# A split-precision decoder trunk: high and low halves of x side by side in one 512-column operand

## The chip, the core and the metric

One core of one Trainium2 chip runs the whole kernel. The metric is the device time of one execution in microseconds (us); lower is better. The kernel before was timed three times: 864.3, 863.32 and 862.85 us, median 863.32.

## The reference

Two layers over 256 tokens of 1024 channels, all in float32. Cut to what matters here:

```python
for l in range(2):
    u = x @ w_in[l]                                   # 1024 -> 7168 columns
    u_conv, dq, dk, dv, mq, mk, mv, g = jnp.split(u, offs, axis=-1)
    y_a = conv_branch(u_conv, ...)                    # a*sigmoid(gt), 31-tap causal conv, layer norm, silu, @ w_conv_out
    y_b = diff_attention(dq, dk, dv, ...)             # rope on q and k, two softmaxes, rms norm, @ w_diff_out
    y_c = moba_attention(mq, mk, mv, ...)             # rope on q and k, softmax, @ w_moba_out
    gates = sigmoid(g + b_gate[l]).reshape(B, S, 3, D)
    m = gates[:, :, 0] * y_a + gates[:, :, 1] * y_b + gates[:, :, 2] * y_c
    x = layer_norm(ALPHA * x + m @ w_o[l], ...)
    h = square(relu(x @ w_ff1[l] + b_ff1[l]))         # 1024 -> 4096
    x = layer_norm(ALPHA * x + h @ w_ff2[l] + b_ff2[l], ...)
```

## The kernel before, in words

**Precision.** Every large product is made of three matmuls on halves: a value is split into a high part (rounded by a cast, on ScalarE) and a low part (the rest, a subtraction on VectorE), and `mm3` (line 391) adds low x high, high x low and high x high in one PSUM bank. Weights come from HBM in pieces of 128 x 1024 (512 KB) on SP's queue, and `Weights.get` (line 341) splits each: `raw` (4 buffers), `whi` and `wlo` (8 each).

**Units.** `tunit` (line 528) computes 256 output channels, channels on the partitions and tokens along the columns: two halves c, each one weight piece, each 8 steps over the input channels (kt). A step is one `mm3` with the weights loaded and x as the moving operand, 256 columns; both halves lie in one bank of tag `pm`. It is used for q and k (8 units in a layer), the gates (12) and most of MLP 1 (13, i from 3 to 15). The evictions: `rope` (line 602) copies four quarters of 32 partitions swapped to SBUF on ScalarE and multiplies and adds on VectorE; a gate takes two Tanh reads with bias; `hsplit` (line 860) two Relu reads with bias, a Square and a split.

**Order of a layer.** Convolution input, v projections, q and k, then the gates and output projections of the three branches in turn: gates and projection of the differential attention (bi 0), of MoBA (bi 1), of the convolution (bi 2); then `w_o` and layer norm 1, MLP 1 and MLP 2 interleaved, layer norm 2. VectorE does the 31 taps of the convolution meanwhile (`tap`, line 552). `conv_ln` (line 757: transposes, statistics, normalisation) stands behind the first gate unit of bi 2, `conv_silu` (line 775: transposes, scale and Tanh on ScalarE, product and split) behind the second. Attention pieces are put between the units by `tick`.

**Who sets the order.** All operations are recorded with guessed costs, and `Plan.order` (line 234) issues them engine by engine: of what could go at a moment, the one with the earliest due time, where due times follow TensorE's recorded order. Every instruction's line is therefore that of `record` (L122). PSUM has three tags: `pm` 2 banks, `pa` 4, `pt` 2.

Of the kernel before, what the change touches and what calls it, by code (L numbers as in the profile page):

```python
# [9 lines left out]
F32 = mybir.dt.float32  # L10
# [15 lines left out]
WARM = 4  # L26
NW = 8
CONV_BIAS = 0
BANKS = {"pm": 2, "pa": 4, "pt": 2}

NCOL = 24 + 4 * TAPS + 4 + 4 + 4 + 1 + 32
# [326 lines left out]
def kernel(ctx: ExitStack, tc: tile.TileContext, x, xT, w_in, w_p2, w_o, w_f1, w_f2,  # L358
# [38 lines left out]
    def at(pair, *ix):  # L397
        return tuple(a[ix] for a in pair)
# [11 lines left out]
    order = []  # L410
    for l in range(L):
        order += [w_in[l, i] for i in range(32)]
        for b in range(3):
            order += [w_in[l, 32 + 8 * b + i] for i in range(8)]
            order += [w_p2[l, 4 * b + i] for i in range(4)]
# [9 lines left out]
    X = [[], []]  # L425
    for h in range(2):
        a, hi, lo = slot(F32, "xt32"), slot(name="xh"), slot(name="xl")
        for q in range(2):
            s = slice(q * 512, (q + 1) * 512)
            R.SP.dma_start(a[:, s], xT[:, h * 1024 + q * 512:h * 1024 + (q + 1) * 512])  # L430
            split(hi[:, s], lo[:, s], a[:, s])
        X[0].append(hi)
        X[1].append(lo)
    cst_t = R.tile(const, [P, 896], F32, "cst", 1)
    R.SP.dma_start(cst_t, cst)
    cosT = cst_t[:, 0:256]
# [15 lines left out]
    def x_new():  # L452
        return [[slot(name="x") for _ in range(2)] for _ in range(2)]

    def x_at(X, kt, cols=slice(0, SEQ)):

        return tuple(X[i][kt // 4][:, (kt % 4) * SEQ + cols.start:(kt % 4) * SEQ + cols.stop]
                     for i in range(2))

    def rstd_of(var, n=1, eps=EPS, scale=1.0):  # L460

# [9 lines left out]
    def ln_tok(t, banks, resid, alpha, gb, dst, transposed):  # L471

        y = slot(F32, "y")
        st = R.tile(small, [P, 2, 6], F32, "st", 2)
        for h in range(2):
            s = slice(h * 512, (h + 1) * 512)
            R.DVE.scalar_tensor_tensor(y[:, s], in0=resid[:, s], scalar=alpha, in1=banks[h],
                                           op0=ALU.mult, op1=ALU.add)
            R.DVE.bn_stats(st[:, h, :], y[:, s])
        mv = col(2, "mv")  # L480
        R.DVE.bn_aggr(mv, st)
        rstd = rstd_of(mv[:, 1:2])
        for h in range(2):
            s = slice(h * 512, (h + 1) * 512)
            R.DVE.scalar_tensor_tensor(y[:, s], in0=y[:, s], scalar=mv[:, 0:1],
                                           in1=gb[0][:, s], op0=ALU.subtract, op1=ALU.mult)
            R.DVE.scalar_tensor_tensor(dst[:, s], in0=y[:, s], scalar=rstd,
                                           in1=gb[1][:, s],
                                           op0=ALU.mult, op1=ALU.add)
            if transposed is not None:  # L490
                ps = bank("pt")
                for k in range(4):
                    R.PE.transpose(ps[:, k * P:(k + 1) * P],
                                        dst[:, h * 512 + k * P:h * 512 + (k + 1) * P], ident)
                hi, lo = [transposed[i][h].rearrange("p (k n) -> p k n", k=4)[
                    :, :, t * P:(t + 1) * P] for i in range(2)]
                split(hi, lo, ps.rearrange("p (k n) -> p k n", k=4))

    def load_row(l, i):
        t = slot(F32, "rows")  # L500
# [3 lines left out]
    for l in range(L):  # L504
# [21 lines left out]


        def tunit(ticks=True):
            ps = bank()
            for c in range(2):  # L530
                w = W.get(k=KT)
                for kt in range(KT):
                    mm3(ps[:, c * 256:(c + 1) * 256], at(w, ALLP, kt), x_at(X, kt), kt == 0,
                        kt == KT - 1)
                if ticks:
                    tick()
            return ps

        attn = deque()
        tickn = [0]  # L540
# [61 lines left out]
        def rope(ps, dst):  # L602
            qq = R.tile(work, [P, 1024], F32, "zz", 3)
            q, qr = qq[:, :512], qq[:, 512:]
            for a in range(0, P, 64):
                R.Activation.copy(qr[a:a + 32], ps[a + 32:a + 64])
                R.Activation.copy(qr[a + 32:a + 64], ps[a:a + 32])
            p3 = ps.rearrange("p (c n) -> p c n", c=2)
# [191 lines left out]

        macc = [None, None]
        M = None
        for bi, gofs in ((0, 8), (1, 16), (2, 0)):
            sg = []
            for u in range(4):
                if u % 2 == 0:
                    sg.append(slot(F32, "sg"))
                ps = tunit()
                for c in range(2):
                    n = 2 * u + c  # L810
                    R.Activation.activation(sg[n // 4][:, (n % 4) * 256:(n % 4 + 1) * 256],
                                         ps[:, c * 256:(c + 1) * 256], AF.Tanh, scale=0.5,
                                         bias=half[:, C_BG + gofs + n:C_BG + gofs + n + 1])
                if bi == 2 and u == 0:
                    xn = conv_ln()
                if bi == 2 and u == 1:
                    conv_silu(xn)
            br = branch(bi)
            if bi == 2:
                M = x_new()  # L820
            for u in range(4):
                w = W.get(c=2, k=4)
                ps = bank()
                for c in range(2):
                    for kt in range(4):
                        mm3(ps[:, c * 256:(c + 1) * 256], at(w, ALLP, c, kt), at(br, ALLP, kt),
                            kt == 0, kt == 3)
                s = slice((u % 2) * 512, (u % 2 + 1) * 512)
                if bi == 0:
                    if u % 2 == 0:  # L830
                        macc[u // 2] = slot(F32, "macc")
                    a = macc[u // 2][:, s]
                    R.DVE.scalar_tensor_tensor(a, in0=sg[u // 2][:, s], scalar=1.0, in1=ps,
                                                   op0=ALU.add, op1=ALU.mult)
                else:
                    a, g = macc[u // 2][:, s], sg[u // 2][:, s]
                    R.DVE.scalar_tensor_tensor(g, in0=g, scalar=1.0, in1=ps, op0=ALU.add,
                                                   op1=ALU.mult)
                    R.DVE.tensor_add(a, a, g)
                    if bi == 2:  # L840
                        split(M[0][u // 2][:, s], M[1][u // 2][:, s], a, 0.5)
                tick()


        gb1 = load_row(l, 0), load_row(l, 1)
# [14 lines left out]
        def hsplit(i, ps):  # L860

            r = R.tile(work, [P, 1024], F32, "zz", 3)[:, :512]
            for c in range(2):
                n = 2 * i + c
                R.Activation.activation(r[:, c * 256:(c + 1) * 256], ps[:, c * 256:(c + 1) * 256],
                                     AF.Relu, bias=C[:, C_BF1 + n:C_BF1 + n + 1])
# [156 lines left out]
```

## Time and profile before

| what | value |
|---|---|
| median of three runs | 863.32 us |
| profiled execution | 864.63 us |
| its span, first to last instruction | 862.9 us |
| TensorE busy | 849.0 us (98%), 5736 matmuls |
| VectorE, ScalarE, GpSimd busy | 623.6, 513.0, 20.6 us |
| mean granted clock of TensorE | 0.998 |
| HBM traffic | 157.06 MB, mean 182 GB/s |

Engines are called PE (TensorE's matmuls), PEld (its weight loads), DVE (VectorE), ACT (ScalarE), POOL (GpSimd) and SP (the DMA queue). Matmuls overlap in their records: one of 256 columns has a record of 0.28 us, but in a run they start 0.12 us apart. The pace is therefore read from start to start, or from a run's length over its count. Busy times are shares of the whole span; what limits a stage is read in that stage.

### The profile page before, as it was taken

To read this page: it belongs to the slowest core of one execution; us is meant where nothing else is said; L and a number is where in the kernel's file an instruction comes from. 1 tells how busy PE (TensorE), PEld (TensorE's weight loads), DVE (VectorE), ACT (ScalarE), POOL (GpSimd) and SP (SyncE) were. 2 spreads that over 40 slices of the span, in tenths; PEclk is the share of its full clock that TensorE was granted. 3 is DMA by queue.
4 is the path that set the end of the run, shared out by engine and by line. 5 is a ranking of instruction groups with operands and counts; after the bars stand their busy time and mean duration, and the time that the engine had idled before them with its cause. 6 is when DMAs were issued, how large, how long until landed. Compare 5 with 4: busy or idle time off the path is not lost.

```text
span 862.9 us, 14667 instructions
## 1 busy us (share of the span) xinstructions
PE 849.0 (98%) x5736; PEld 779.1 (90%) x5736; DVE 623.6 (72%) x1011; ACT 513.0 (59%) x854; POOL 20.6 (2%) x26
## 2 busy tenths in 40 slices
PE   8999999999999999999999999999999999999996
PEld 7899999999988999999887999999998899999995
DVE  5899999985696654454688999998766874454445
ACT  5578997447347555555344688965472675555540
POOL 0000110000000000000000001000000000000000
PEclk9999999999999999999999999999999999999999
DMA  8874435565537765555265744355553686565521
GB/s 330 281 253 153 149 100 171 171 191 159 189 143 249 268 194 185 185 189 182 94 209 162 261 148 133 118 164 183 186 171 123 219 293 201 190 195 182 187 72 49
DMA packets 44421, 157.06 MB, mean 182 GB/s; under 512 B 4928, under 2 KB 5440, under 8 KB 44352
## 3 DMA queue, kind: packets, MB, share of 16 engines
q1 hardware_dynamic: 44352, 156.13, 54.4%
q8 instruction: 45, 0.74, 0.3%
q14 instruction: 24, 0.20, 0.1%
HBM read 155.06 MB, written 1.05 MB: 181 GB/s over the span
## 4 chain that ended last, share of the span: by engine, by line
PE 87%; DVE 7%; ACT 2%; DMA 2%; issue 1%; POOL 1%; DVEq 0%; ACTq 0%
PE pm L122 55%; PE pa L122 31%; ACT zz L122 2%; DVE wlo L122 2%; DVE big L122 1%; DVE zz L122 1%; DVE pt L122 1%; POOL col L122 1%; DMA raw<-in_w_f_dram 1%; DMA raw<-in_w_in_dram 1%; PE pt L122 1%; DVE qk L122 1%; ACT whi L122 0%; DMA big<-in_xT_dram 0%; DVE col L122 0%
## 5 line engine op out<-in xcount | busy, mean ns | idle before, releaser
L122 PE MATMUL pm<-big,whi 128*128 128x256 f32 x2496 | 452.6, 283 | 0.0
L122 DVE TENSOR_TENSOR wlo<-raw,whi 128x1024 fp32r<-128x1024 f32 (+1 forms) x283 | 341.4, 1210 | 153.6 <-ACT whi L122 152.1
L122 ACT CAST whi<-raw 128x1024 fp32r<-128x1024 f32 (+1 forms) x283 | 294.0, 1043 | 241.5 <-PE pm L122 170.8
L122 PEld LDWEIGHTS pm<-big,whi 128*128 128x128 f32 x2496 | 388.8, 192 | 1.2
L122 PE MATMUL pm<-big,wlo 128*128 128x256 f32 x1248 | 356.9, 286 | 0.0
L122 PEld LDWEIGHTS pm<-big,wlo 128*128 128x128 f32 x1248 | 239.0, 191 | 4.0 <-ACT pt L122 0.3
L122 PE MATMUL pa<-whi,big 128*128 128x512 f32 x704 | 224.8, 392 | 1.1 <-DVE big L122 1.1
L122 PEld LDWEIGHTS pa<-whi,big 128*128 128x128 f32 x704 | 132.8, 189 | 28.7 <-ACT whi L122 1.8
L122 PE MATMUL pa<-wlo,big 128*128 128x512 f32 x352 | 137.9, 392 | 0.0
L122 DVE SCALAR_TENSOR_TENSOR big<-hpad,half,big 128x256 f32<-128x256 f32 x240 | 103.3, 475 | 0.1
L122 PE MATMUL pm<-whi,big 128*128 128x512 f32 (+1 forms) x320 | 92.5, 370 | 0.0
L122 PEld LDWEIGHTS pa<-wlo,big 128*128 128x128 f32 x352 | 66.6, 189 | 12.7
L122 PEld LDWEIGHTS pm<-whi,big 128*128 128x128 f32 x320 | 58.3, 188 | 10.3 <-ACT zz L122 0.4
L122 PE MATMUL pm<-wlo,big 128*128 128x512 f32 (+1 forms) x160 | 59.3, 372 | 0.0
L122 ACT COPY zz<-pm 32x512 f32<-32x512 f32 (+1 forms) x72 | 40.8, 567 | 9.5 <-DVE zz L122 4.9
L122 DVE TENSOR_TENSOR big<-zz,big 128x512 fp32r<-128x512 f32 x32 | 22.1, 691 | 27.8 <-ACT big L122 27.8
L122 ACT ACTIVATE pt<-pt,col 128x256 f32<-128x256 f32 (+1 forms) x96 | 41.4, 459 | 0.7 <-DVE col L122 0.3
L122 POOL TENSOR_TENSOR col<-col,mhalf 128x1 f32<-128x1 f32 (+1 forms) x20 | 20.0, 1001 | 785.3 <-DVE col L122 785.3
L122 PEld LDWEIGHTS pm<-wlo,big 128*128 128x128 f32 x160 | 30.2, 189 | 4.8
L122 ACT CAST big<-pt 128x512 fp32r<-128x512 f32 x12 | 6.9, 591 | 37.7 <-PE pt L122 37.5
L122 DVE SCALAR_TENSOR_TENSOR big<-big,pa 128x512 f32<-128x512 f32 x16 | 11.0, 685 | 19.7 <-PE pa L122 19.5
L122 ACT ACTIVATE zz<-pm,cols 128x256 f32<-128x256 f32 x52 | 21.6, 465 | 4.7 <-PE pm L122 4.7
(79 smaller groups left out, 446.9 us busy)
## 6 DMA issues: line engine op xcount, KB each, us to landing
raw<-in_w_f_dram SPq DMA_DIRECT2D x128, 512.0 KB, 3.7
raw<-in_w_in_dram SPq DMA_DIRECT2D x109, 512.0 KB, 3.6
raw<-in_w_p_dram SPq DMA_DIRECT2D x24, 512.0 KB, 3.4
raw<-in_w_o_dram SPq DMA_DIRECT2D x16, 512.0 KB, 3.4
big<-in_rows_dram SPq DMA_DIRECT2D x10, 512.0 KB, 6.1
raw<-in_w_in_dram SPq DMA_DIRECT2D x6, 256.0 KB, 5.2
big<-in_xT_dram SPq DMA_DIRECT2D x4, 256.0 KB, 5.3
big<-in_x_dram SPq DMA_DIRECT2D x2, 512.0 KB, 8.2
```

The lines of the kernel that those rows point to most:

```text
L122: op.fn = lambda: fn(*args, **kw)
```

## The change

`x_new`, `x_at` and two new helpers lay x out so that for each kt the high and the low 256 columns stand side by side. In `tunit` a step becomes two matmuls: the high weights with all 512 columns (high and low x), and the low weights with the 256 high columns. The two halves of a bank are then added when they are read: `tsum` reads the upper half on ScalarE (with the bias) and adds the lower half on VectorE. Each half c of a unit takes a bank of its own, c = 0 of tag `pm`, c = 1 of `pt`. Relu and Tanh follow on the sum, 512 columns at a time. The gates of all branches stay recorded as before, but the order becomes gates 0, projection 0, gates 1, gates 2, `conv_ln`, projection 1 with `conv_silu` behind its second unit, projection 2. Weights are fetched in that order. The outputs of the splits after a norm and after the merge are written in two pieces or in three dimensions.

```diff
+GATED = (("gate", 0), ("out", 0), ("gate", 1), ("gate", 2), ("out", 1), ("out", 2))
...
+    def x_both(X, kt):
+
+        return X[kt // 2][:, (kt % 2) * 512:(kt % 2 + 1) * 512]
...
     for h in range(2):
-        a, hi, lo = slot(F32, "xt32"), slot(name="xh"), slot(name="xl")
+        a = slot(F32, "xt32")
         for q in range(2):
             s = slice(q * 512, (q + 1) * 512)
             R.SP.dma_start(a[:, s], xT[:, h * 1024 + q * 512:h * 1024 + (q + 1) * 512])
-            split(hi[:, s], lo[:, s], a[:, s])
+            split(*x_pair(X, 2 * h + q), a[:, s].rearrange("p (k n) -> p k n", k=2))
...
-                split(hi, lo, ps.rearrange("p (k n) -> p k n", k=4))
+                p4 = ps.rearrange("p (k n) -> p k n", k=4)
+                for j in range(2):
+                    split(*x_pair(transposed, 2 * h + j, slice(t * P, (t + 1) * P)),
+                          p4[:, 2 * j:2 * j + 2])
...
         def tunit(ticks=True):
-            ps = bank()
+            out = []
             for c in range(2):
                 w = W.get(k=KT)
+                ps = bank(("pm", "pt")[c])
                 for kt in range(KT):
-                    mm3(ps[:, c * 256:(c + 1) * 256], at(w, ALLP, kt), x_at(X, kt), kt == 0,
-                        kt == KT - 1)
+                    hi, lo = at(w, ALLP, kt)
+                    R.PE.matmul(ps, hi, x_both(X, kt), start=kt == 0, stop=False)
+                    R.PE.matmul(ps[:, 0:SEQ], lo, x_at(X, kt)[0], start=False,
+                                stop=kt == KT - 1)
+                out.append(ps)
...
+        def tsum(dst, ps, bias):
+
+            if bias is None:
+                R.Activation.copy(dst, ps[:, SEQ:])
+            else:
+                R.Activation.activation(dst, ps[:, SEQ:], AF.Identity, bias=bias)
+            R.DVE.tensor_add(dst, dst, ps[:, 0:SEQ])
...
         def rope(ps, dst):
...
+            for c in range(2):
+                tsum(q[:, c * 256:(c + 1) * 256], ps[c], None)
             for a in range(0, P, 64):
-                R.Activation.copy(qr[a:a + 32], ps[a + 32:a + 64])
-                R.Activation.copy(qr[a + 32:a + 64], ps[a:a + 32])
+                R.Activation.copy(qr[a:a + 32], q[a + 32:a + 64])
+                R.Activation.copy(qr[a + 32:a + 64], q[a:a + 32])
...
-            R.DVE.tensor_mul(q3, p3, cb)
+            R.DVE.tensor_mul(q3, q3, cb)
...
+                for c in range(2):
+                    n = C_BG + gofs + 2 * u + c
+                    tsum(g[:, c * 256:(c + 1) * 256], ps[c], C[:, n:n + 1])
+                R.Activation.activation(g, g, AF.Tanh, scale=0.5)
...
+        gates(0)
+        outs(0)
+        gates(1)
+        gates(2)
+        xn = conv_ln()
+        outs(1, lambda: conv_silu(xn))
+        M = x_new()
+        outs(2)
...
+                if i < 3:
+                    R.Activation.activation(rc, ps[:, c * 256:(c + 1) * 256], AF.Relu, bias=b)
+                else:
+                    tsum(rc, ps[c], b)
+            if i >= 3:
+                R.Activation.activation(r, r, AF.Relu)
```

**What the planner makes of it, at two places.** First TensorE at the start of the conv branch's output projection in layer 0. `big_465` and `big_466` are the high and low half of that branch before the change, `big_492` and `big_493` behind it; `whi` and `wlo` are the weights' halves. Before:

```order
L122 MATMUL pm_493<-big_465,wlo_492 128x256
L122 MATMUL pm_493<-big_466,whi_491 128x256
L122 MATMUL pm_493<-big_465,whi_491 128x256
L122 MATMUL pm_493<-big_465,wlo_492 128x256
L122 MATMUL pm_493<-big_466,whi_491 128x256
```

With the change:

```order
L123 MATMUL pm_505<-big_360,whi_503 128x256
L123 MATMUL pm_505<-big_359,whi_503 128x256
L123 MATMUL pm_513<-big_492,wlo_512 128x256
L123 MATMUL pm_517<-big_492,wlo_516 128x256
L123 MATMUL pm_513<-big_493,whi_511 128x256
L123 MATMUL pm_513<-big_492,whi_511 128x256
```

Two units of the projection (`pm_513`, `pm_517`) now alternate, and the first matmul of each needs the high half alone. The transposes of `conv_silu` stand in the MoBA projection, 28 matmuls ahead of the first of these rows with `pm_513`; in layer 1, 33 matmuls. Before, 91 matmuls lie between in layer 0.

Second, SP's queue at the very start. `big_75` and `big_78` are the first and second half of xT before the change. Before:

```order
L122 DMA big_75<-in_xT_dram 128x512
L122 DMA raw_95<-in_w_in_dram 128x512 x2
L122 DMA big_75<-in_xT_dram 128x512
L122 DMA raw_98<-in_w_in_dram 128x512 x2
L122 DMA raw_101<-in_w_in_dram 128x512 x2
L122 DMA big_78<-in_xT_dram 128x512 x2
L122 DMA raw_104<-in_w_in_dram 128x1024
```

With the change, where `big_79` and `big_80` are the halves of xT:

```order
L123 DMA big_79<-in_xT_dram 128x512
L123 DMA raw_95<-in_w_in_dram 128x512 x2
L123 DMA big_79<-in_xT_dram 128x512
L123 DMA raw_98<-in_w_in_dram 128x512 x2
L123 DMA raw_101<-in_w_in_dram 128x512 x2
L123 DMA raw_104<-in_w_in_dram 128x1024
L123 DMA cst_81<-in_cst_dram 128x896
L123 DMA big_80<-in_xT_dram 128x512 x2
```

The second half of xT has moved behind a weight piece (512 KB) and the constants (448 KB).

## Rows read from the trace of the kernel before

**Rows 1.** The page, chain that ended last: shares of the span by engine.

```profile
PE 87%; DVE 7%; ACT 2%; DMA 2%; issue 1%; POOL 1%; DVEq 0%; ACTq 0%
```

**Rows 2.** TensorE's waits: waiter, for whom, us in total, times, longest us.

```profile
PE pa L122 <- DVE big L122: 2.1, 3, 1.1
```

**Rows 3.** The chain in order of time: start us, length us, what, instructions.

```profile
18.75 10.88 PE pm L122 x48
...
202.87 22.43 PE pm L122 x187
...
307.08 5.75 PE pm L122 x48
312.83 5.47 PE pa L122 x24
```

**Rows 4.** Timeline of TensorE in the MLP: start us, record us, instruction, count.

```profile
306.69 0.39 PE L122 MATMUL pa<-whi,big 128*128 128x512 f32 x1
306.92 0.28 PE L122 MATMUL pm<-big,wlo 128*128 128x256 f32 x1
...
312.43 0.40 PE L122 MATMUL pm<-big,whi 128*128 128x256 f32 x2
312.67 0.40 PE L122 MATMUL pa<-whi,big 128*128 128x512 f32 x1
```

**Rows 5.** Groups by shape: count, then busy us, mean ns of one, idle before.

```profile
L122 ACT COPY zz<-pm 32x512 f32<-32x512 f32 x64 | 37.0, 578 | 5.9 <-DVE zz L122 4.9
L122 ACT ACTIVATE zz<-pm,cols 128x256 f32<-128x256 f32 x52 | 21.6, 465 | 4.7 <-PE pm L122 4.7
L122 ACT ACTIVATE zz<-zz 128x512 f32<-128x512 f32 x32 | 20.5, 640 | 0.8
L122 DVE TENSOR_TENSOR big<-pt,big 128x512 fp32r<-128x512 f32 x12 | 8.0, 687 | 3.3 <-ACT big L122 3.3
L122 ACT CAST big<-pt 128x512 fp32r<-128x512 f32 x12 | 6.9, 591 | 37.7 <-PE pt L122 37.5
L122 DVE TENSOR_TENSOR big<-pa,big 64x256 fp32r<-64x256 f32 x16 | 6.7, 420 | 0.1
L122 ACT COPY zz<-pm 128x256 f32<-128x256 f32 x4 | 1.5, 370 | 3.1 <-PE pm L122 3.1
```

**Rows 6.** Windows: length us; PE, PEld, DVE, ACT, POOL busy us; clock; DMA.

```profile
60.00:110.00 50.00, 49.42 (x411) 47.77 (x410) 45.53 (x112) 42.92 (x93) 3.23 (x2) 1.00 0.49 162
110.00:140.00 30.00, 29.96 (x247) 28.12 (x247) 29.37 (x83) 29.76 (x88) 2.15 (x2) 1.00 0.42 134
140.00:195.00 55.00, 55.00 (x462) 54.03 (x459) 51.12 (x87) 25.93 (x38) 0.20 (x1) 1.00 0.54 176
...
280.00:400.00 120.00, 120.00 (x769) 109.64 (x768) 62.41 (x56) 65.50 (x88) 0.00 (x0) 1.00 0.63 203
```

**Rows 7.** Timeline of VectorE, layer 0: the last taps of the convolution.

```profile
174.52 3.25 DVE L122 SCALAR_TENSOR_TENSOR big<-hpad,half,big 128x256 f32<-128x256 f32 x8
```

**Rows 8.** Timeline, layer 0: `conv_silu`'s last transposes and the split of its result.

```profile
202.05 0.82 PE L122 MATMUL pa<-cst,big 128*128 128x128 f32 x6
...
207.71 0.68 DVE L122 SCALAR_TENSOR_TENSOR big<-zz,big 128x512 fp32r<-128x512 f32 x1
...
209.82 0.69 DVE L122 SCALAR_TENSOR_TENSOR big<-zz,big 128x512 fp32r<-128x512 f32 x1
```

**Rows 9.** Timeline of the start: second half of xT, the weights behind it, TensorE.

```profile
10.92 1.26 ACT L122 CAST big<-big 128x512 fp32r<-128x512 f32 x2 [0.61 <-DMA big<-in_xT_dram]
...
11.58 1.33 DVE L122 TENSOR_TENSOR big<-big,big 128x512 fp32r<-128x512 f32 x2 [0.53 <-ACT big L122]
...
12.85 1.05 ACT L122 CAST whi<-raw 128x1024 fp32r<-128x1024 f32 x1 [0.67 <-DMA raw<-in_w_in_dram]
12.92 0.62 PE L122 MATMUL pa<-whi,big 128*128 128x512 f32 x2
...
14.12 1.05 ACT L122 CAST whi<-raw 128x1024 fp32r<-128x1024 f32 x1 [0.22 <-DMA raw<-in_w_in_dram]
```

More of the change, by code (lines that the diff above doesn't have):

```diff
@@ L412 @@
         order += [w_in[l, i] for i in range(32)]
-        for b in range(3):
-            order += [w_in[l, 32 + 8 * b + i] for i in range(8)]
-            order += [w_p2[l, 4 * b + i] for i in range(4)]
+        for step, b in GATED:
+            if step == "gate":
+                order += [w_in[l, 32 + 8 * b + i] for i in range(8)]
+            else:
+                order += [w_p2[l, 4 * b + i] for i in range(4)]
         order += [w_o[l, i] for i in range(8)]
@@ L424, with x_new, x_pair, x_at @@
     W = Weights(R, wpool, order)
-    X = [[], []]
+    def x_new():
+        return [slot(name="x") for _ in range(4)]
+    def x_pair(X, j, cols=slice(0, SEQ)):
+        a = X[j].rearrange("p (k n) -> p k n", k=2)
+        return tuple(a[:, :, i * SEQ + cols.start:i * SEQ + cols.stop] for i in range(2))
+    def x_at(X, kt, cols=slice(0, SEQ)):
+        o = (kt % 2) * 512
+        return tuple(X[kt // 2][:, o + i * SEQ + cols.start:o + i * SEQ + cols.stop]
+                     for i in range(2))
+    def x_both(X, kt):
+        return X[kt // 2][:, (kt % 2) * 512:(kt % 2 + 1) * 512]
+    X = x_new()
     for h in range(2):
-        a, hi, lo = slot(F32, "xt32"), slot(name="xh"), slot(name="xl")
+        a = slot(F32, "xt32")
         for q in range(2):
@@ L450 @@
         xtok.append(a)
[L452 to L458, printed above, removed]
     def rstd_of(var, n=1, eps=EPS, scale=1.0):
@@ L528, in tunit @@
         def tunit(ticks=True):
-            ps = bank()
+            out = []
             for c in range(2):
                 w = W.get(k=KT)
+                ps = bank(("pm", "pt")[c])
                 for kt in range(KT):
-                    mm3(ps[:, c * 256:(c + 1) * 256], at(w, ALLP, kt), x_at(X, kt), kt == 0,
-                        kt == KT - 1)
+                    hi, lo = at(w, ALLP, kt)
[3 more added lines that the diff above has]
+                out.append(ps)
                 if ticks:
                     tick()
-            return ps
+            return out
+        def tsum(dst, ps, bias):
[4 more added lines that the diff above has]
+            R.DVE.tensor_add(dst, dst, ps[:, 0:SEQ])
         attn = deque()
@@ L802, with gates, outs @@
         M = None
-        for bi, gofs in ((0, 8), (1, 16), (2, 0)):
-            sg = []
+        SG = {}
+        def gates(bi):
+            gofs = (8, 16, 0)[bi]
+            SG[bi] = []
             for u in range(4):
                 if u % 2 == 0:
-                    sg.append(slot(F32, "sg"))
+                    SG[bi].append(slot(F32, "sg"))
                 ps = tunit()
+                g = SG[bi][u // 2][:, (u % 2) * 512:(u % 2 + 1) * 512]
                 for c in range(2):
[L810 to L820, printed above, removed]
+                    n = C_BG + gofs + 2 * u + c
+                    tsum(g[:, c * 256:(c + 1) * 256], ps[c], C[:, n:n + 1])
+                R.Activation.activation(g, g, AF.Tanh, scale=0.5)
+        def outs(bi, hook=None):
+            br, sg = branch(bi), SG[bi]
             for u in range(4):
@@ L827 @@
                             kt == 0, kt == 3)
+                if hook and u == 1:
+                    hook()
                 s = slice((u % 2) * 512, (u % 2 + 1) * 512)
@@ L840 @@
                     if bi == 2:
-                        split(M[0][u // 2][:, s], M[1][u // 2][:, s], a, 0.5)
+                        split(*x_pair(M, u), a.rearrange("p (k n) -> p k n", k=2), 0.5)
                 tick()
+        gates(0)
[6 more added lines that the diff above has]
+        outs(2)
         gb1 = load_row(l, 0), load_row(l, 1)
@@ L864, in hsplit @@
                 n = 2 * i + c
-                R.Activation.activation(r[:, c * 256:(c + 1) * 256], ps[:, c * 256:(c + 1) * 256],
-                                     AF.Relu, bias=C[:, C_BF1 + n:C_BF1 + n + 1])
+                b = C[:, C_BF1 + n:C_BF1 + n + 1]
+                rc = r[:, c * 256:(c + 1) * 256]
+                if i < 3:
+                    R.Activation.activation(rc, ps[:, c * 256:(c + 1) * 256], AF.Relu, bias=b)
+                else:
+                    tsum(rc, ps[c], b)
+            if i >= 3:
+                R.Activation.activation(r, r, AF.Relu)
             R.Activation.activation(r, r, AF.Square)
```

5 lines of the change are left out of this document (removed).

## The prediction, made blind

> **What bounds the kernel now.** I read the chain of waits first, then TensorE's own waits, then its pace in the stages that change, and last the engines that evict. The chain that ends last is 87% TensorE [rows 1], and TensorE's longest sum of waits is 2.1 us in three places, all for a bank that VectorE has not yet emptied [rows 2]. So the time is TensorE's instruction stream, and a change pays by what it takes out of that stream, as long as ScalarE and VectorE keep ahead.
>
> **The pace.** In a conv-projection run 48 matmuls of 512 columns take 10.88 us, 226.7 ns each; in an MLP unit 48 matmuls of 256 columns take 5.75 us, 119.8 ns each [rows 3]. Twice 256 columns cost 239.6 ns, once 512 cost 226.7: every matmul pays 12.9 ns beyond its columns. The timeline shows the mixed step too: the 256-column matmul after a 512-column one starts 0.23 us later, the 512-column one after a run of 256 starts 0.12 us later [rows 4]. So a pair 512 + 256 should take 226.7 + 119.8 = 346.5 ns where three of 256 take 359.4.
>
> **Part 1, TensorE.** A unit of `tunit` has 2 x 8 steps. There are 8 units for q and k, 12 for gates and 13 for MLP 1 in a layer, 33, so 2 x 33 x 16 = 1056 steps. Each saves 12.9 ns: **-13.6 us**. With the 5.47 us for 24 in the MLP [rows 3], 227.9 ns each, it would be 1056 x 11.7 = 12.4.
>
> *Against it stands a rule.* The Trainium skill (TensorE: Matmul & The Clock Gate, Back-to-back issue gap) gives a warm gap of N / 2.4 ns plus about 2.5 ns. By it a step would save 2.5 ns and the part 2.6 us instead of 13.6. The row disagrees for this stream (119.8 ns at 256 columns), and I go by the row.
>
> **Part 2, the evictions.** Each half unit gets a ScalarE read of its upper half and a VectorE add of its lower half. The nearest rows are 0.370 us (copy of 256 columns) and 0.420 us (add from a bank, 256 columns) [rows 5]. A rope unit gets 2 copies and 2 adds, and its four quarter copies now read SBUF (some 0.04 us more each, if at all): ScalarE 2 x 0.370 + 0.16 = 0.90 us, VectorE 0.84. A gate unit exchanges two Tanh of 256 for two Identity (0.465) and one Tanh of 512 (0.640): ScalarE +0.61, VectorE +0.84. An MLP unit gets a Relu of 512: the same.
>
> - *MLP.* VectorE is busy 62.4 and ScalarE 65.5 of 120 us [rows 6], about 5.8 and 6.1 of each period of 11.2. They grow to 6.7 and 6.7. TensorE's own stream covers that: nothing. A bank comes round again after three other half units, over 8 us.
> - *Rope and attention.* Here there is little cover. ScalarE is busy 42.9 of 50 and then 29.8 of 30 us, VectorE 45.5 and 29.4 [rows 6]. Until the first branch projection a layer adds 8 x 0.90 + 4 x 0.61 = 9.6 us to ScalarE, while TensorE's part shrinks by 12 x 16 x 12.9 ns = 2.5 us; the idle there is 7.3 us. So 9.6 + 2.5 - 7.3 = 4.8 us must move to a later place. Some can: the MoBA branch is now needed only after all gates. Ends: from -1.2 (even the present waits go) to 2 x 4.8 = +9.6. I take **+2.0**, near the row of TensorE's waits (2.1), since in the new order TensorE's whole blocks of 16 still stand between the attention pieces there, with one piece split.
> - *Convolution taps.* They end at 177.8 us [rows 7]; ropes and gates put 20 x 0.84 = 16.8 us of adds on the same engine, so 194.6 if none finds a gap (idle from 60 to 195: 9.0 us [rows 6]). Of the 187 matmuls after 202.87 the first 91 lie ahead of the conv projection (`w_p2` of the conv branch), so that starts at 202.87 + 10.9 = 213.8 [rows 3]. The norm's transposes now come one projection (96 x 0.12 = 11.5 us) and the transposes' own 0.9 ahead of that place, and 20 units x 16 x 12.9 ns = 4.1 us sooner by part 1: at 197.3. Covered by 2.7 us: nothing. Without the cover each microsecond goes straight into the wait of part 3.
>
> **Part 3, the norm moved behind the gates.** No instruction is removed, but the distance shrinks. Before, 91 matmuls (10.9 us) lie between the last transposes of `conv_silu` and the conv projection. Now those transposes stand inside the MoBA projection, and 28 matmuls follow them in layer 0, 33 in layer 1: 3.4 and 4.0 us. The work between is 8 ScalarE reads, a product, a cast and a subtraction. In the trace the last transposes start at 202.05 and the run behind them at 202.87, the first low half is done at 207.71 + 0.68 = 208.4 and the second at 209.82 + 0.69 = 210.5 [rows 3, 8]: 5.5 and 7.6 us after the transposes. ScalarE's reads are in a row in both orders, so this cannot shrink much. TensorE waits 5.5 - 3.4 = 2.1 us in layer 0 and 5.5 - 4.0 = 1.5 in layer 1; there the second half comes at 7.6, while TensorE is through the first after 4.0 + 1.5 + 12 x 0.12 = 6.9, another 0.7 (in layer 0 the new order has no weight subtraction between the halves on VectorE, so nothing more): **+4.3**. Ends: 0 (if the transposes get there early) and 8.4 (if it starts 2 us later in each layer). That the written order lets two projections alternate there is its own sign of a wait. Queued behind: TensorE's next 192 matmuls; nobody else loses.
>
> **Part 4, the start.** The second half of xT is moved behind a weight (512 KB) and the constants (448 KB) on SP's queue. The weights behind it are cast at 12.85 and 14.12, each as it lands: 1.27 us for 512 KB, so the half comes up to 1.27 + 1.11 = 2.4 us later. Its VectorE pair began at 11.58; the first result comes at 11.58 + 0.7 + 2.4 = 14.7. TensorE reaches it after 24 matmuls, about 13.15 (second of the pair at 12.92) [rows 9]: **+1.5**, ends 0 and 2.4.
>
> **Part 5, the split after a norm.** One cast of 0.591 and one subtraction of 0.687 become two of each of half size (about 0.37 and 0.42) [rows 5]: the first low half comes sooner, the last at 0.37 + 0.27 + 0.13 + 0.42 = 1.2 instead of 1.4 us. Three norms pass it: **-0.3**, ends -1.0 and +0.5. The three-dimensional outputs are the same number of elements: nothing. The four slots of gate values that now live together are covered by the order of the row loads, which stays: nothing.
>
> **Sum.** -13.6 + 2.0 + 4.3 + 1.5 - 0.3 = -6.1 us. The profiled execution took 864.6, so 858.5 by it; it stands 1.3 above the median of three (863.3), so I predict **857.2**.
>
> **The rivals.**
> - *All waits are covered*: ScalarE reads ahead and parts 2 to 5 cost 0 to 4 us. For it: TensorE waits almost nowhere now. Against: the distances of part 3 are counted, not guessed. 863.3 - 13.6 = 849.7, up to 855.
> - *ScalarE becomes the bound* (slower): between the first rope and the first projection its idle time is itself waiting for data and can't be filled. The break-even is (13.6 + 0.3 - 4.3 - 1.5) / 2 = 4.05 us exposed in a layer. With the 4.8 us of part 2 in full: 863.3 - 8.1 + 9.6 = 864.8. With all 7.2 us of the rope evictions: 863.3 - 8.1 + 14.4 = 869.6. For it: 29.8 busy of 30. Against: MoBA work can go later.
> - *The step doesn't shrink* (slower): a 512-column matmul with x as the moving operand costs what two of 256 cost; the trace has 512 columns only with weights moving [rows 4]. Then the change adds work for nothing: 863.3 + 7.5 = 870.8. The gap of the Trainium skill (TensorE: Matmul & The Clock Gate, Back-to-back issue gap) would come near this, with 868.2; the trace speaks against it.
> - *The norm's move costs nothing or even helps*: then -10.4 and 852.9, inside the first rival's neighbourhood.
>
> **Chances.** Forecast, 855 to 860: 0.52. Waits covered, below 855: 0.24. Somewhat worse waits, 860 to 861.6: 0.07. ScalarE the bound: 0.13, of which 0.08 ends within 0.2% (1.7 us, about what this measurement can tell) and 0.05 above. The step doesn't shrink: 0.04. So faster 0.83, same 0.08, slower 0.09. The range 850.5 to 862.0 takes in most of the first two and leaves out about 0.08 below and 0.12 above.
>
> **What would show it.** Right: TensorE has 1056 matmuls fewer; a unit of 32 matmuls takes 5.54 us instead of 5.75; TensorE waits about 2 us for `big` (the conv branch) at the start of each conv projection, and 1 to 2 us near 13 us. Wrong: a unit still at 5.7 us (part 1 falls); ScalarE as the end of TensorE's waits between 60 and 140 us of more than 8 us in all (part 2 falls); no wait ahead of the conv projection (part 3 falls).

## The result: slower, by 0.64%

The change takes 869.85 us (median of 4) where the kernel before takes 863.38 on the same chip, 6.5 us less. The ratio on record, by which all runs are compared here, is 1.0064 (5.5 us), with a 95% interval from 1.0052 to 1.0076. 857.2 us was forecast, with at most 862.0. The profiled execution has a span of 867.4 us, 4.5 more than that of before. The ledger of waits below accounts for these 4.5 us; the rest of the difference between the medians isn't located.

### The profile after

First the page: the busy line, the chain that ended last, and TensorE's groups for the units that changed.

```profile
PE 844.9 (97%) x4680; PEld 722.2 (83%) x4680; DVE 667.1 (77%) x1155; ACT 553.9 (64%) x948; POOL 18.0 (2%) x26
PE 75%; ACT 12%; DVE 6%; DMA 4%; issue 2%; POOL 0%; SPq 0%; DVEq 0%; ACTq 0%
L123 PE MATMUL pt<-big,whi 128*128 128x512 f32 x528 | 192.3, 403 | 0.0
L123 PE MATMUL pt<-big,wlo 128*128 128x256 f32 x528 | 148.8, 282 | 0.0
```

The change does what it says: 5736 - 4680 = 1056 matmuls fewer. But TensorE's share of the chain falls from 87% [rows 1] to 75%, and ScalarE's rises from 2% to 12%. Both follow the releasers that the profile infers, and one of these is not what TensorE waited for, as the timelines below show. TensorE's own waits name ScalarE first (waiter, for whom, us in total, times, longest us), where before VectorE stood at the top with 2.1 us [rows 2] and ScalarE came second with 1.5:

```profile
PE pa L123 <- ACT big L123: 2.3, 2, 1.3
PE pa L123 <- DVE big L123: 2.3, 1, 2.3
PE pa L123 <- ACT zz L123: 1.9, 3, 1.0
PE pm L123 <- DVE big L123: 1.7, 3, 0.8
PE pa L123 <- DVE col L123: 1.5, 3, 0.6
```

The chain in order of time gives the pace and, where both kernels have the same piece of work, a milestone (start us, length us, what, instructions). After:

```profile
19.90 10.88 PE pm L123 x48
150.93 5.94 PE pm L123 x48
229.86 15.45 PE pa L123 x68
276.92 5.48 PE pa L123 x24
289.27 2.81 PE pm L123 x16
292.08 2.83 PE pt L123 x16
576.85 5.94 PE pm L123 x48
655.66 15.44 PE pa L123 x68
702.82 5.48 PE pa L123 x24
842.98 16.36 PE pa L123 x72
```

An MLP unit is 2.81 + 2.83 = 5.64 us, where before had 5.75 [rows 3] and 5.54 was forecast. A step is 5.64 / 16 = 352.5 ns and saves 6.9, not 12.9.

The same pieces of the chain of before, less the first, which stands in [rows 3] (18.75):

```profile
147.52 5.94 PE pm L122 x48
225.29 15.44 PE pa L122 x68
272.03 5.47 PE pa L122 x24
572.48 5.94 PE pm L122 x48
650.25 15.44 PE pa L122 x68
696.71 5.47 PE pa L122 x24
838.49 16.36 PE pa L122 x72
```

Between two milestones both kernels do the same matmuls, so the lag of the change can be read stage by stage. Only ahead of the first MLP 2 run the change has two thirds of a step more (12 steps where before has 34 of 36 matmuls), 0.23 us, and so much less behind it. Taken out of the lag are these and what the faster steps give, steps x 6.9 ns. What is left is waiting, with the slower pace that follows some waits.

| up to this piece | lag | grew by | faster steps | moved | waits added |
|---|---|---|---|---|---|
| second run of the convolution input (19.90) | +1.15 | +1.15 | 0 | 0 | 1.15 (start) |
| first projection, layer 0 (150.93) | +3.41 | +2.26 | 192: -1.32 | 0 | 3.58 (attention) |
| `w_o`, layer 0 (229.86) | +4.57 | +1.16 | 128: -0.88 | 0 | 2.04 (conv branch) |
| first MLP 2 run, layer 0 (276.92) | +4.89 | +0.32 | 12: -0.08 | +0.23 | 0.17 |
| first projection, layer 1 (576.85) | +4.37 | -0.52 | 388: -2.68 | -0.23 | 2.39 (attention) |
| `w_o`, layer 1 (655.66) | +5.41 | +1.04 | 128: -0.88 | 0 | 1.92 (conv branch) |
| first MLP 2 run, layer 1 (702.82) | +6.11 | +0.70 | 12: -0.08 | +0.23 | 0.55 |
| last run (842.98) | +4.49 | -1.62 | 196: -1.35 | -0.23 | 0.0 |

Sum: 1.15 (start) + 5.97 (attention) + 3.96 (conv branch) + 0.72 (from `w_o` to MLP 2) - 7.27 (steps) = +4.5 us.

Where the attention waits, layer 0, timeline of TensorE (start us, record us, instruction, count, idle before and who ended it):

```profile
135.08 0.38 PE L123 MATMUL pa<-cst,o 128*128 128x128 f32 x2
136.76 0.52 PE L123 MATMUL pa<-cst,pt 128*128 128x128 f32 x3 [1.30 <-ACT big L123]
137.89 0.52 PE L123 MATMUL pa<-cst,pt 128*128 128x128 f32 x3 [0.61 <-DVE col L123]
...
139.04 0.63 PE L123 MATMUL pt<-big,whi 128*128 128x512 f32 x1
139.47 0.41 PE L123 MATMUL pt<-big,wlo 128*128 128x256 f32 x1
...
142.24 0.39 PE L123 MATMUL pt<-big,whi 128*128 128x512 f32 x1
```

ScalarE in the same stretch:

```profile
134.39 0.78 ACT L123 CAST big<-pa 64x256 fp32r<-64x256 f32 x2
135.19 1.04 ACT L123 CAST whi<-raw 128x1024 fp32r<-128x1024 f32 x1
136.26 0.47 ACT L123 ACTIVATE big<-pt,cols 128x256 f32<-128x256 f32 x1
136.63 0.47 ACT L123 ACTIVATE big<-pm,cols 128x256 f32<-128x256 f32 x1
```

And the window behind it (length, busy us of PE, PEld, DVE, ACT and POOL, granted clock, DMA share, GB/s):

```profile
139.40:142.10 2.70, 2.70 (x10) 2.24 (x9) 2.70 (x8) 2.70 (x10) 0.00 (x0) 0.50 0.04 14
```

Two transposes, then two waits, and ScalarE without a gap: casts of weights and of the attention's result, then two added reads of a gate unit (`big<-pt,cols`, `big<-pm,cols`). The profile puts the first wait down to such a read, since that ends just ahead of the start. But the transposes use nothing that it makes. They write a bank of `pa`, and the read of such a bank that ends last ahead of them is VectorE's subtraction from the MoBA branch's result (`big<-pa`), at 136.61. It stands behind a weight's subtraction:

```profile
134.63 1.22 DVE L123 TENSOR_TENSOR wlo<-raw,whi 128x1024 fp32r<-128x1024 f32 x1
135.76 0.85 DVE L123 TENSOR_TENSOR big<-pa,big 64x256 fp32r<-64x256 f32 x2
```

ScalarE's cast of the same result was through at 134.39 + 0.78 = 135.17. So the last link of this wait is VectorE, in the order that the planner gave it, and not ScalarE's read.

After these two waits the granted clock is 0.50, the lower of its two levels (1.2 GHz). The five steps from 139.04 to 142.24 take 3.20 us instead of 5 x 0.3525 = 1.76. So the lower clock costs another 1.4 us here, which no part of the prediction had; the 3.58 us of the table hold it. The waits alone don't decide it: e1 below, which has the same operations up to the MLP, has them too (1.36 us at 136.63 and 0.61 at 137.76) and keeps its clock:

```profile
139.00:142.00 3.00, 3.00 (x21) 2.19 (x21) 3.00 (x8) 3.00 (x11) 0.00 (x0) 1.00 0.08 26
```

There the clock is at 0.50 from 219 to 221 us, behind the waits of the conv branch, where the change keeps 1.00. What makes it fall behind one wait and not behind another isn't shown.

### The profile page after: what moved, and what is told of

It reads as the page before. It is cut to its first block, busy times and chain, and to the rows that moved or that the text cites. A ratio compares the mean times of both kernels' runs of the same rounds, so it can differ in the third digit from the quotient of the medians.

```text
span 867.4 us, 12709 instructions
## 1 busy us (share of the span) xinstructions
PE 844.9 (97%) x4680; PEld 722.2 (83%) x4680; DVE 667.1 (77%) x1155; ACT 553.9 (64%) x948; POOL 18.0 (2%) x26
## 4 chain that ended last, share of the span: by engine, by line
PE 75%; ACT 12%; DVE 6%; DMA 4%; issue 2%; POOL 0%; SPq 0%; DVEq 0%; ACTq 0%
PE pm L123 31%; PE pa L123 27%; PE pt L123 18%; ACT zz L123 3%; ACT pt L123 3%; ACT whi L123 3%; DMA raw<-in_w_f_dram 3%; DVE wlo L123 2%; DVE big L123 2%; ACT big L123 2%; DMA raw<-in_w_in_dram 1%; ACT o L123 1%; DMA big<-in_xT_dram 1%; DVE zz L123 0%; ACT ptT L123 0%
## 5 line engine op out<-in xcount | busy, mean ns | idle before, releaser
L123 PE MATMUL pm<-big,whi 128*128 128x512 f32 (+1 forms) x912 | 260.4, 351 | 1.7 <-DVE big L123 1.7
L123 PE MATMUL pm<-big,wlo 128*128 128x256 f32 x720 | 203.4, 283 | 0.8 <-ACT big L123 0.7
L123 PE MATMUL pt<-big,whi 128*128 128x512 f32 x528 | 192.3, 403 | 0.0
L123 PEld LDWEIGHTS pm<-big,whi 128*128 128x128 f32 x912 | 158.9, 189 | 27.1 <-DVE big L123 2.7
L123 PE MATMUL pt<-big,wlo 128*128 128x256 f32 x528 | 148.8, 282 | 0.0
L123 PEld LDWEIGHTS pm<-big,wlo 128*128 128x128 f32 x720 | 136.3, 189 | 2.9 <-ACT big L123 1.2
L123 PEld LDWEIGHTS pt<-big,whi 128*128 128x128 f32 x528 | 100.1, 190 | 24.3
L123 PEld LDWEIGHTS pt<-big,wlo 128*128 128x128 f32 x528 | 100.4, 190 | 0.1
L123 PEld LDWEIGHTS pa<-wlo,big 128*128 128x128 f32 x352 | 66.1, 188 | 12.9 <-DVE wlo L123 0.4
L123 ACT ACTIVATE zz<-zz 128x512 f32<-128x512 f32 x58 | 36.7, 634 | 31.8 <-DVE zz L123 31.6
L123 ACT COPY zz<-zz 32x512 f32<-32x512 f32 x64 | 39.6, 618 | 2.1 <-DVE zz L123 1.0
```

The costliest lines, as they stand in the source:

```text
L123: op.fn = lambda: fn(*args, **kw)
```

## The experiments

Each timed run has its own runs of the kernel before on the same chip (medians 863.4 to 864.7 us), so ratios are compared. 0.0010 is 0.86 us, and the intervals are some 1 to 2 us wide to either side.

| run | ratio to before | 95% interval |
|---|---|---|
| the change | 1.0064 | 1.0052 to 1.0076 |
| e2, old order | 0.9981 | 0.9971 to 0.9992 |
| e3, new order alone | 1.0043 | 1.0029 to 1.0057 |
| e4, MLP only | 1.0007 | 0.9997 to 1.0016 |
| e6, old order, grouped | 0.9935 | 0.9921 to 0.9950 |
| e7, e6 with the old q and k | 1.0003 | 0.9992 to 1.0014 |
| e8, e6 with xT early | 0.9920 | 0.9907 to 0.9933 |
| e9, grouped over a whole unit | 0.9977 | 0.9963 to 0.9990 |
| e10, upper half not read in q, k, gates | 0.9991 | 0.9980 to 1.0002 |
| e11, e8 with rope's copy on VectorE | 0.9921 | 0.9905 to 0.9936 |
| e12, the change, grouped | 0.9992 | 0.9981 to 1.0003 |
| e13, e8 with half of the copies on VectorE | 0.9912 | 0.9890 to 0.9934 |

### The step: why 352.5 ns and not 346.5

The matmuls of one half unit in other orders (`high` has 512 columns, `low` 256):

```diff
 # A, as changed
 for kt in range(KT): high(kt); low(kt)
+# B
+for kt in range(KT): high(kt)
+for kt in range(KT): low(kt)
+# C: low adds to ps[:, SEQ:] instead of ps[:, 0:SEQ]
+# E: high, low, low, high, high, low, ...
+# G: both half units in turns: high 0, high 1, low 0, low 1
```

> The changed kernel, with the 32 matmuls of an MLP 1 unit (13 units a layer) written in five orders, the numbers computed being the same: A as changed (512, 256, 512, 256, ...); B the eight of 512 columns of a half unit first, then the eight of 256; C as A, but the 256-column product is added to the upper half of the bank instead of the lower; E the order turned in every second step (512, 256, 256, 512, ...); G the two half units taken in turns (512, 512, 256, 256 over two banks). Before this run a step of A takes 352 ns (235 + 117) in the profile of the change, where 346.5 was forecast. Theory 1, the change from one width to the other is what costs: B takes 8 x 227 + 8 x 120 = 2.77 us for a half unit, E between, A and C 2.82. Theory 2, x as the 512-column moving operand costs 235 ns wherever it stands: B 8 x 235 + 8 x 118 = 2.82, all five alike. Theory 3, adding at once to the columns that the matmul before has just written costs: C and G 2.77, A and E 2.82 or more, B 2.77. The whole run is one look: 869.9 less at most 26 x 5 x 0.05 / 13 = 1 us by any of them.

e1 ran once: 866.76 us, with 864.68 for before. Its span of 864.5 us is 2.9 shorter than the change's, of which the faster units explain 1 us; its other waits and its clock differ too. It serves for the paces alone. In the chain, with units in the orders B, C, E, A one after the other (two rows each):

```profile
287.85 2.77 PE pm L123 x16
290.61 2.79 PE pt L123 x16
...
298.88 2.81 PE pm L123 x16
301.69 2.83 PE pt L123 x16
...
309.98 2.78 PE pm L123 x16
312.76 2.79 PE pt L123 x16
...
320.99 2.81 PE pm L123 x16
323.81 2.83 PE pt L123 x16
```

B takes 2.77 and 2.79, as theory 1 gives, although x moves in all of it: theory 2 is out. C (298.88) takes the same as A (320.99), and the unit in order G, over two banks, takes 5.56 us in all, like E, which stays in one: theory 3 is out. So it is the alternation of widths that costs. But it has no fixed price per change: E has half as many changes as A and loses 0.01 us a unit to B, where A loses 0.08. Two of one width in a row already save nearly all. In the trace's starts the first 256-column matmul behind one of 512 is followed after 113 ns and the 512-column ones behind one of 256 after 230 to 241, while runs of one width settle at 227 and 120. B's second half unit, behind eight of 256, pays some 0.02 us once. Why TensorE does this the profile doesn't say; that stays open.

Then the whole change in order B:

```diff
 for kt in range(KT):
     R.PE.matmul(ps, at(w, ALLP, kt)[0], x_both(X, kt), start=kt == 0, stop=False)
-    R.PE.matmul(ps[:, 0:SEQ], at(w, ALLP, kt)[1], x_at(X, kt)[0], ...)
+for kt in range(KT):
+    R.PE.matmul(ps[:, 0:SEQ], at(w, ALLP, kt)[1], x_at(X, kt)[0], ...)
```

> The change itself, new order, with nothing but the order within a half unit turned to eight of 512 and then eight of 256 columns. Theory: 132 x 0.045 = 5.9 us less, of which e6_grouped kept 4.0 beside e2_old_order; so 1.0064 becomes 0.9995 to 1.002 of before. Rival, all of it comes back as waits for the attention and the conv branch: 1.004 or more.

1.0064 became 0.9992: 0.0072, or 6.2 us, against 5.9 expected. This alone makes the change no slower than before. A step is then 2.78 / 8 = 347.5 ns and saves 11.9, near the forecast. That the whole comes out so near is partly luck, since the waits moved too: the wait at 136.52 is 1.74 us here, with the clock held, and the granted clock is 0.50 from 216 to 218 and from 540 to 543 us.

Beside the old order of gates and projections (e2, below):

> The old order of gates and projections (as e2_old_order), and in every half unit the eight matmuls of 512 columns first, then the eight of 256 (order B of e1_step_orders). Theory, the change of width within the step ate half of the gain: 132 half units save 2.825 - 2.78 = 0.045 us, 5.9 in all, so e2_old_order's 0.9981 of before becomes 0.9913 (857 us where before is 864.7). Rival, the time that TensorE saves comes back as waits for the attention's ScalarE and VectorE work or for weights: between 858.5 and 862.7.

0.9981 to 0.9935, 4.0 us of the 5.9. The rest came back as waits. In layer 1 TensorE now starts a MoBA transpose at 556.70 after 1.7 us. The profile names ScalarE again; what ends just ahead of it in the banks `pa` is VectorE's read of attention scores (`pt<-pa,cst`, 556.26 + 0.28), behind a weight's subtraction and the add of a gate unit.

Grouping further, over both half units:

```diff
+for c in range(2):
+    for kt in range(KT): high(c, kt)
+for c in range(2):
+    for kt in range(KT): low(c, kt)
```

> As e6_grouped, but grouped over a whole unit: the sixteen matmuls of 512 columns of both half units (two banks), then the sixteen of 256. Theory: one change of width per unit instead of two, each worth some 25 ns in e1_step_orders (a half unit that begins on 512 takes 2.77, one that follows on 256 takes 2.79): 66 units save 1.6 us against e6_grouped. Rival, the first bank is now given out later and both weights are needed at once, so waits for evictions or weights take it back: no difference or slower.

Slower than e6 by 3.6 us. The pace was had, and lost to waits of 2.3 us at the start, 2.1 us at 120.10 and 1.8 us at 542.66, the latter two before attention scores. Neither theory named these places. Behind all three the granted clock is 0.50 (from 15 to 17, 121 to 127 and 544 to 546 us), where that of e6 is 1.00 on average from 10 to 850. So the waits alone would have cost less. (The profiled run, 864.04 us, lies above the median of 861.71.)

### The order of gates and projections

The new order alone, in the kernel before (`GATED` and `gates`/`outs` as in the change, the rest as before):

> The kernel before with the new order of gates and projections alone, operand and evictions as before. Theory: 3.4 to 4.3 us of waits ahead of the conv projections as in the change, 863.4 + 3.8 = 867.2. Rival, the waits come only because ScalarE and VectorE carry the added evictions: then 863 to 864.

1.0043, 3.7 us. The waits stand where they were expected, in both layers alike; layer 0, timeline:

```profile
214.56 0.50 PE L123 MATMUL pm<-big,whi 128*128 128x256 f32 x2 [0.43 <-DVE big L123]
...
216.90 0.51 PE L123 MATMUL pm<-big,whi 128*128 128x256 f32 x2 [0.52 <-DVE big L123]
```

The chain reaches `w_o` of layer 0 at 227.00 instead of 225.29 and the last run at 842.02 instead of 838.49: 1.7 and 1.8 us a layer. Each shows 0.43 or 0.52 us of idle time, but the start that follows is 0.69 us late.

The change in the old order:

```diff
-        gates(0); outs(0); gates(1); gates(2)
-        xn = conv_ln()
-        outs(1, lambda: conv_silu(xn))
+        gates(0); outs(0); gates(1); outs(1)
+        gates(2, True)   # conv_ln behind its first unit, conv_silu behind its second
```

> The changed kernel with the old order: each branch's gates right ahead of its projection, the norm and the activation of the convolution inside the conv gates. Theory: the order costs what the trace of the change shows ahead of the two conv projections, 0.86 + 0.94 us in layer 0 and 0.25 + 0.69 + 0.68 in layer 1, 3.4 in all, so 869.85 - 3.4 = 866.4. Rival, the order pays for something else (the MoBA branch comes later, so ScalarE's added reads have a place): then those waits go and others come between 120 and 200 us, and the time stays at 869 to 871 or goes up.

0.9981, that is 7.2 us faster than the change and not 3.4. The waits ahead of the conv projections go (TensorE is idle 0.2 us from 200 to 225 and not at all from 625 to 650), and so do those at 136.76 and 137.89 with the drop of the clock. In layer 1 waits remain (2.2 us idle from 485 to 570), and the clock is at 0.50 from 540 to 543. So order and evictions are not additive. Up to the first projection both kernels have the same operations, and e2 has the same added reads. But there VectorE's subtraction `big<-pa` starts at 134.10, right behind taps of the convolution and with no weight's subtraction ahead of it. That order is the planner's choice, by due times that the new order moves for the MoBA branch; that it makes the whole difference isn't shown.

### The evictions

The cost taken away:

```diff
-tsum(q[:, c * 256:(c + 1) * 256], ps[c], None)
+R.DVE.tensor_copy(q[:, c * 256:(c + 1) * 256], ps[c][:, 0:SEQ])
...
-tsum(gc, ps[c], C[:, n:n + 1])        # and one Tanh of 512
+R.DVE.tensor_copy(gc, ps[c][:, 0:SEQ])
+R.Activation.activation(gc, gc, AF.Tanh, scale=0.5, bias=half[:, n:n + 1])
```

> The changed kernel, new order, with ScalarE's added reads in q, k and gates taken away: VectorE copies the lower half of the bank where it added both halves, ScalarE does the two Tanh of 256 columns as before, from SBUF. It leaves out the product of W's high part and x's low part in q, k and gates. VectorE's instructions and TensorE's stream are those of the change. Theory, ScalarE is what the attention of the change waits for: TensorE's excess over its pace falls from 4.1 to under 0.5 us between 125 and 150 us, from 2.9 to under 0.5 between 550 and 575, and some below 125; 5 to 7 us faster than the change, 0.998 to 1.000 of before. Rival, the waits come from the new order or from VectorE's adds: within 1.5 us of the change, 1.005 or more.

0.9991, 6.3 us faster than the change, with the amount of VectorE's and TensorE's work unchanged. The same place in its timeline:

```profile
133.47 0.38 PE L123 MATMUL pa<-cst,o 128*128 128x128 f32 x2
133.69 0.49 PE L123 MATMUL pa<-cst,pt 128*128 128x128 f32 x3
134.71 0.52 PE L123 MATMUL pa<-cst,pt 128*128 128x128 f32 x3 [0.54 <-DVE col L123]
134.99 0.48 PE L123 MATMUL pt<-big,whi 128*128 128x512 f32 x1
135.30 0.28 PE L123 MATMUL pt<-big,wlo 128*128 128x256 f32 x1
```

The wait of 1.30 us is gone, the 0.54 behind VectorE stays, and the clock holds here. (It falls later, to 0.50 from 215 to 217 us, ahead of the conv projection.) Windows of the attention say the same in sums:

| window, us | engine | before | change | e2 | e3 | e10 |
|---|---|---|---|---|---|---|
| 60 to 140 | TensorE idle | 0.6 | 2.4 | 1.2 | 0.4 | 0.6 |
| 485 to 570 | TensorE idle | 0.4 | 2.6 | 2.2 | 0.8 | 0.7 |
| 60 to 140 | ScalarE busy | 72.7 | 77.1 | 77.1 | 72.7 | 75.1 |

So the added reads cost these waits, although VectorE stood last in them; the order alone (e3) makes hardly any here. How the reads do it stays partly open: with them go ScalarE's time, VectorE's wait for each read ahead of its add, and the planner's order on both engines. That ScalarE's time counts is borne out by e11 below, where VectorE has more to do and TensorE has no idle time in either window.

The operand in the MLP alone (`tunit_old` is the `tunit` of before, with its evictions, for q, k and gates):

```diff
-                    ps = tunit()
+                    ps = tunit_old()
...
-                ps = tunit()
+                ps = tunit_old()
```

> The old order, and the 512-column operand with its evictions in MLP 1 alone; q, k and gates with three matmuls of 256 into one bank and evicted as before; x laid out in pairs, and so loaded as in the change. Theory: 416 steps save 7 ns each as the trace of the change shows, -2.9 us, the late second half of xT costs 1.2 at the start, the MLP evictions cost nothing: 863.4 - 2.9 + 1.2 = 861.7. Rival, the evictions cost in the MLP too (VectorE and ScalarE behind TensorE's banks): 863.5 or more.

1.0007, 2.3 us above the theory. Its chain shows why: it is 2.0 us late already at the first projection (149.56), loses nothing in the conv branch, and wins 1.0 in the last stretch from `w_o` of layer 1 to the last run (651.57 to 838.80, where before takes 650.25 to 838.49). So MLP evictions are hidden, as forecast, and the start and the first attention eat the small gain.

The operand everywhere but in q and k, on e6:

> e6_grouped, with q and k (8 units a layer, 256 steps in all) back to three matmuls of 256 columns into one bank and the rope read straight from the bank as before. Theory: 256 x (359.4 - 347.5) ns = 3.0 us more on TensorE, and the waits of the attention go back to what before had, 2.0 to 2.5 us less, so within 1.5 us of e6_grouped. Rival, the rope evictions are covered: 3 us slower than e6_grouped. Rival, they cost more than the steps save: 1 us or more faster than e6_grouped.

5.9 us slower than e6, more than any of the three gave. ScalarE is less loaded here (70.8 busy us between 60 and 140, e6 78.3), and still TensorE waits 2.06 us for it at 118.09, ahead of attention scores that need the bank which the copy `ptT` empties. ScalarE's order in e7:

```profile
112.82 1.76 ACT L123 COPY zz<-pm 32x512 f32<-32x512 f32 x3
...
115.44 0.58 ACT L123 COPY zz<-pm 32x512 f32<-32x512 f32 x1
...
117.55 0.48 ACT L123 COPY ptT<-pa 128x384 f32<-128x384 f32 x1
```

All four quarter copies of a rope unit, 2.3 us, stand in the 5 us ahead of that copy; in e6 one of them does (110.54) and the wait there is 0.37 us. So the order on ScalarE, which the planner makes from guessed costs, decided here, not its load. In layer 1 e7 waits 2.18 us at 541.57, and behind both waits its clock is at the lower level (granted 0.51 from 120 to 123 and 0.50 from 544 to 546 us), which e6 hasn't. What the operand for q and k is worth by itself stays open.

Rope's copy moved to the other engine, on e8:

```diff
-                R.Activation.copy(dst, ps[:, SEQ:])
+                R.DVE.tensor_copy(dst, ps[:, SEQ:])
```

> e8_grouped_xT_early with the copy of the upper half in rope on VectorE instead of ScalarE, 16 x 0.37 us in a layer less on ScalarE, 16 x 0.42 us more on VectorE, whose convolution taps have room until the conv gates. Theory, ScalarE is short in the attention: the waits of 0.6 to 1.9 us at 113, 134, 534 and 557 us shrink by half or more, 2 to 3 us faster than e8_grouped_xT_early, 0.989. Rival, VectorE is as short: no difference or up to 4 us slower.

No difference to e8: the first part of the theory held (TensorE has no idle time at all from 60 to 140 and from 485 to 570), and the rival too. VectorE is now behind, and the wait stands ahead of `w_o`:

```profile
225.90 0.80 PE L123 MATMUL pa<-whi,big 128*128 128x512 f32 x1 [2.59 <-DVE big L123]
```

Half of the copies moved:

```diff
+            if vector:                      # the first of the two half units
+                R.DVE.tensor_copy(dst, ps[:, SEQ:])
```

> e8_grouped_xT_early with the copy of the upper half in rope on VectorE for the first of the two half units and on ScalarE for the second. e11 (all on VectorE) took the waits of the attention away and made new ones of 2.7 and 1.7 us ahead of w_o. Theory, the two engines share a budget and a half share leaves neither wait whole: under 1 us at 226 and 646 us, about half of e8's waits at 113, 134, 534 and 557, together 1 to 2 us faster than e8, 0.990 to 0.991. Rival, each microsecond only moves from the one to the other: 0.992, no difference.

0.9912 beside 0.9920, inside both intervals: undecided. The wait ahead of `w_o` of layer 0 stays at 2.6 us, that of layer 1 doesn't come.

### The start

Both slots for xT are taken first, then filled and split:

```diff
-    for h in range(2):
-        a = slot(F32, "xt32")
-        for q in range(2): ...dma_start(a...); split(...)
+    halves = [slot(F32, "xt32") for _ in range(2)]
+    for h in range(2):
+        for q in range(2): ...dma_start(halves[h]...)
+    for h in range(2):
+        for q in range(2): split(...)
```

> e6_grouped, with both slots that receive xT taken ahead of the slots of the split x, so that the second half's transfers are not held back until the first half has been split. Theory: the transfers go out ahead of the constants and the fourth whole weight, TensorE's wait near 14 us goes, and the time falls by 1 to 1.5 us against e6_grouped. Rival, the weights behind come as much later and TensorE waits for those instead: no difference.

0.9935 to 0.9920, 1.3 us; the intervals overlap, but the chain's second run of the convolution input starts at 18.54 instead of 19.47, and the wait near 14 us is gone. In the planner a tile gets its slot in the order of first use. With x laid out in pairs, the second slot for xT stood behind one for the split x that is first written from the second quarter, so its transfer couldn't be issued. That is the cause of the moved transfers, not a due time.

e8 beats both kernels: 856.87 us against 863.9 of before on that chip. e13 has the lowest median, 855.67 (before there: 863.63).

## Why the prediction was wrong, point by point

- **The bound** (TensorE's stream, as long as ScalarE and VectorE keep ahead) was right, and its condition failed: in the attention ScalarE, and VectorE behind it, don't keep ahead.
- **Part 1, -13.6 us: wrong, -7.3.** The step that failed is "a pair 512 + 256 should take 226.7 + 119.8 = 346.5 ns". Both paces came from long runs of one width; the two transitions of [rows 4] that were to confirm the sum are printed to 0.01 us, while what was at stake was 6 ns in each of 1056 steps. e1 and e12 show that the sum holds when widths don't alternate. Measured were savings of 6.9 ns a step alternating and 11.9 grouped: the pace of the rows holds only in runs. By the rule weighed there (Trainium skill, TensorE: Matmul & The Clock Gate, Back-to-back issue gap) a step would have saved 2.5 ns. The Trainium skill gives that formula there for an isolated matmul and not for a stream of them, which the prediction leaves out, and neither 6.9 nor 11.9 agrees with it.
- **Part 2, evictions +2.0: right in kind, too small.** 6.0 us of waits, inside the ends -1.2 and +9.6. The failing step is the choice near the waits of before, argued with "Some can: the MoBA branch is now needed only after all gates". MoBA's result is needed later, but its transposes keep their place in TensorE's order, between the gate units. TensorE, which keeps that order, waits at that place, however late the result is needed. The row of 2.1 us that the choice leant on was misread: 1.15 of it is the first matmul at 6.11 waiting for the split of xT, not for a bank, and only 0.58 and 0.32 us lie in the attention. The MLP at nothing was right (e4), the taps were right: the conv projections' waits are those of e3. Nor did it have the lower clock behind one wait, 1.4 of the 6.0 us.
- **Part 3, norm +4.3: right.** 4.0 by the milestones, 3.7 by e3. But undoing it gave 7.2 in e2, since it also changes what the attention waits for.
- **Part 4, start +1.5: right.** +1.15 by the milestones: the second half sets the time (14.16, forecast 14.7). TensorE's wait is longer, 2.3 us in one piece, since it starts 0.24 us earlier and its first 24 matmuls take 5.9 us instead of 7.0.
- **Part 5, split -0.3:** the stretches from `w_o` to MLP 2 gained 0.2 and 0.55 us of waits instead. What in them is the split was not tried.
- **The rivals.** "ScalarE becomes the bound" came nearest, with 3.6 and 2.4 us in the layers and VectorE as the last link of most waits; with the whole gain of part 1 that would still have been a faster kernel. "The step doesn't shrink" came near the time (870.8) for a wrong reason: the step shrinks, by half of what was forecast. The range missed since the two errors, 6.3 and 4.0 us, point the same way and each was given its own chance alone. None of the three signs of being wrong came: 5.64 us a unit lies between the 5.54 and the 5.7 that were named.

Together: forecast -6.1 = -13.6 + 2.0 + 4.3 + 1.5 - 0.3; found -7.3 + 6.0 + 4.0 + 1.15 + 0.7 = +4.5.

## What to carry to other kernels

Time the sequence that you will write, not its parts: runs of one width and an alternation of widths had different paces here, and splitting one loop into two was worth 6.2 us. Where an engine runs in order, ask of each small piece between its large blocks which engines feed it and what they are given ahead of it; a later need of the result is no slack. Where a profile names the releaser of a wait, ask whether the waiting instruction uses what that one makes. When one engine is relieved by another of nearly the same load, look for the wait at the next place where the other is needed (e11), before counting a gain.

## What the runs showed of the hardware that was not expected

- Alternating matmuls of 512 and 256 columns take 352.5 ns a pair; in twos (order E, 5.57 us a unit) they take 348, eight and eight of them 347.5. The place of the sums in the bank and the bank itself (orders C and G) make no difference.
- Eight transposes with two waits (1.30 and 0.61 us) among them were followed by a stretch at the lower clock (granted clock 0.50) that cost 1.4 us. The same piece with waits of 1.36 and 0.61 us in e1 was not (1.00 from 139 to 142 us).
